# One decoder layer on one core: the ones of the squares from every head group, the fourth sum of x formed beside the second, and the first covering gate tile woven into the end of stick-breaking

## The chip, the core and the metric

The kernel runs on one core of a Trainium2 chip. The metric is the device time of one execution in microseconds (us). PE is TensorE, DVE is VectorE, ACT is ScalarE, POOL is GpSimd and SP is SyncE, which here issues DMAs.

## The reference

Hidden size 1024, 2048 tokens with 16 meta tokens ahead of them, one layer. Cut to its core:

```python
xn = rms_norm(h, norm_gain)
sb_q, sb_k, sb_v, sw_q, sw_k, sw_v, sb_z, sw_z, g_sb, g_sw = split(xn @ w_in)
o_sb = stick_breaking_attention(sb_q, sb_k, sb_v, valid)      # 8 heads of 64
o_sw = sliding_window_sink_attention(rope(sw_q), rope(sw_k), sw_v, sinks, valid)  # 16 heads, 2 of k and v, window 128
y_sb = (o_sb * silu(sb_z)) @ w_branch_sb
y_sw = (o_sw * silu(sw_z)) @ w_branch_swa
merged = sigmoid(g_sb) * y_sb + sigmoid(g_sw) * y_sw
h = h + merged @ w_out
return rms_norm(h, final_norm_gain)[:, BLOCK:]
```

Stick-breaking attention weighs key s for query t by sigmoid(z) times the product of (1 − sigmoid(z)) over the keys between them. Everything is in float32.

## The kernel before

**Numbers and tiles.** A float32 value is split into a high and a low part that PE can multiply at full rate; a product is three matmuls (high·high, low·high, high·low) of 128x128 weights on 128x512 values. `gemm` (L415 to L417) issues them for one column tile of 128 outputs and one group of 512 tokens: 8 steps of the inner dimension, so 24 matmuls into one PSUM bank. The banks are asked for by letter: g, z and t have two buffers each, o and zm one each. A buffer that is asked for again must first have been read by whoever uses its old content.

**Stages.** The tokens are worked in two halves of two groups each, first groups 2 and 3 ("half 0"), then 0 and 1 ("half 1"). In a half come the sliding window with the projections woven in, then stick-breaking attention with gate tiles woven in, then "pairs". A gate tile (`gate`, L583 the sigmoid, which empties the bank) is one column tile of the gates or of z, for both groups: two half-tiles of 24 matmuls, in this stage both in bank g.

**Stick-breaking** (`stick`) is a generator. Per step it makes scores (L1063, bank z), their sigmoid (ACT, L1066), a running product (DVE scans, L1073 and L1075), and five steps later (LT) transposes the rows on PE (L1091, bank t; of the meta tokens L1101). The transposed weights leave bank t split into a high part (ACT, wth, L115) and a low part (DVE, wtl, L116), and then multiply the values (L1122, bank o; of the meta tokens L1116, bank zm). When a head is done, L1126 (ACT) copies the result and L1127 and L1129 (DVE) add it up. `weave` issues one triple of gate matmuls after so much of the stick's work, in proportion to a ratio worked out from costs, so that PE always has something to do while ACT and DVE work.

**Squares.** In half 0, the stick also sums the squares of x for the tokens of the other half (ACT, L1041, two for a head group), into which a column of ones goes as a scale. It is made on POOL (L1080) from the last product row, so that the scheduler can't move the squares ahead of that row. It comes after every second head group; two buffers hold the loaded pieces of x (xq).

**Pairs.** The remaining gate tiles go two at a time by a scheme of seven products in place of eight (`gate_pair`, `seven`, PE L688). It needs sums of quarters of x, t1 to t4 (`sums_of_x`): L601 adds the high and the low part of a piece, L614, L615 and L617 make t3, t2 and t1, and each sum is split in two: L606 the cast on ACT, L607 the rest on DVE. t4 is made in a second phase by two subtractions (L626, L627), and its split stands inside the first pair (`between`). While the sums are made, PE works on covering tiles: 3 gate tiles in half 0 and 2 in half 1, each with the first group's half-tile in bank g and the second's in bank z. Ahead of the pairs their weights are made of sums too (`pair_weights`, L650 to L658).

**What sets the order.** PE's order is the order in which the program is written, by hand. DVE's is written by hand in the start and in the first pair. The order on ACT, DVE and POOL is otherwise set by the framework's scheduler; at run time each engine takes its list in order, and an instruction that waits holds up what follows it.

Of the kernel before, what the change touches and what calls it, by code (L numbers as in the profile page):

```python
# [12 lines left out]
ALU = mybir.AluOpType  # L13
# [6 lines left out]
KT = D // P  # L20
# [8 lines left out]
PLAIN = 18  # L29
# [4 lines left out]
HS = True  # L34
SR = (1.05, 1.09)
ULAG = 3
AB = 6
QW = 6.0
C_SBQ, C_SBK, C_SBV, C_SWQ, C_SWK, C_SWV, C_SBZ, C_SWZ, C_GSB, C_GSW = (
# [3 lines left out]
def f32(ap):  # L43
    return ap.bitcast(F32)
# [3 lines left out]
def tile_kernel(ctx, tc, x, xt, meta, metat, gain, w_in, w_sb, w_sw, w_out, sinks, fgain,  # L48
# [6 lines left out]
    V, A, G, T = nc.vector, nc.scalar, nc.gpsimd, nc.tensor  # L55
# [74 lines left out]

    clock = [0.0]

    def weave(main, side, ratio, credit=0.0):

        for c in main:
            clock[0] += c
            credit = min(credit + c * ratio, 6.0)
            while credit > 0:
                n = next(side, None)
                if n is None:  # L140
                    credit = float("-inf")
                    break
                if n == 0:
                    credit = 0.0
                    break
                credit -= n
        return credit
# [5 lines left out]
    def drain(*gens):  # L153
        for _ in chain(*gens):
            pass
# [433 lines left out]
    def sums_of_x(bp, groups):  # L589

        g, g2 = groups
        b = {"11": (g, 0), "12": (g2, 0), "21": (g, KT // 2), "22": (g2, KT // 2)}
        q = {n: [t[i][:, k:k + KT // 2, :] for t in (xh, xl)] for n, (i, k) in b.items()}
        for t in ("s4h", "s4l"):
            bp.tile([P, KT // 2, P], F32R, tag=t, name=t, bufs=2)
        for n in ("t4", "t1", "t3", "t2"):
            q[n] = [bp.tile([P, KT // 2, GT], F32R, tag=n + e, name=n + e) for e in "hl"]

        def whole(n, k):
            t = tmp()  # L600
            V.tensor_tensor(t, f32(q[n][0][:, k, :]), f32(q[n][1][:, k, :]), op=ALU.add)  # L601
            return t

        def parted(n, k, t):
            h, l = (u[:, k, :] for u in q[n])
            A.copy(h, t)  # L606
            V.tensor_tensor(l, t, f32(h), op=ALU.subtract)  # L607

        ks = range(KT // 2)
        held = [], []  # L610
        for k in ks:
            b11, b12, b22 = (whole(n, k) for n in ("11", "12", "22"))
            t3, t1 = ring_x(), ps(("t", "t", "o", "zm")[k])
            V.tensor_tensor(t3, b22, b12, op=ALU.subtract)  # L614
            V.tensor_tensor(b22, t3, b11, op=ALU.add)  # L615
            parted("t2", k, b22)
            V.tensor_tensor(t1, b12, b11, op=ALU.subtract)  # L617
            held[0].append(t1)
            held[1].append(t3)
        yield q  # L620
        for n, ts in zip(("t1", "t3"), held):
            for k in ks:
                parted(n, k, ts[k])
        for k in ks:
            b21, (t2h, t2l) = whole("21", k), (f32(t[:, k, :]) for t in q["t2"])
            V.tensor_tensor(b21, b21, t2h, op=ALU.subtract)  # L626
            V.tensor_tensor(b21, b21, t2l, op=ALU.subtract)  # L627
            held[0].append(b21)
        yield q
        for k, t in zip(ks, held[0][KT // 2:]):  # L630
            parted("t4", k, t)
        yield q

    def pair_weights(bp, ca, cb, plain):
# [44 lines left out]
            w[n], w[n2] = ([u[:, c] for u in t] for c in (lo, hi))  # L679
        return w  # L680

    def seven(w, b, tag, use, lead, between):

        def product(acc, n, m, first, last):
            (wh, wl), (bh, bl) = w[n], b[m]
            for k in range(KT // 2):
                for i, (l, r) in enumerate(((wh, bh), (wh, bl), (wl, bh))):
                    T.matmul(acc, lhsT=l[:, k, :], rhs=r[:, k, :], start=first and k == i == 0,  # L688
                             stop=k == KT // 2 - 1 and i == 2, skip_group_check=not (first and last))
        a0, p1 = ps("g"), tmp()  # L690
        product(a0, "11", "11", True, lead)
        A.copy(p1, a0)
        if lead:
            a3 = ps(tag)
            product(a3, "12", "21", True, True)
            t = tmp()
            V.tensor_tensor(t, a3, p1, op=ALU.add)
        yield
        a1, a2 = ps("z"), ps("t")
        u2, u3 = tmp(), tmp()  # L700
        product(a1, "s2", "t2", True, False)
        V.tensor_tensor(u2, a1, p1, op=ALU.add)
        if lead:
            between()
            use(0, 0, t)
            yield
        else:
            product(a0, "12", "21", False, True)
            use(0, 0, a0)
        a3 = ps(tag)  # L710
        product(a2, "s1", "t1", True, False)
        product(a1, "s3", "t3", False, True)
        V.tensor_tensor(u3, a1, p1, op=ALU.add)
        product(a3, "22", "t4", True, True)
        V.tensor_tensor(p1, a2, u3, op=ALU.add)
        V.tensor_tensor(u3, a3, u3, op=ALU.add)
        use(1, 1, p1)
        use(1, 0, u3)
        yield
        product(a2, "s4", "22", False, True)  # L720
        V.tensor_tensor(u2, a2, u2, op=ALU.add)
        use(0, 1, u2)

    def gate_pair(bp, ga, gb, groups, q, tag, plain, lead, between):
        tiles = ga, gb

        def use(m, n, t):
            c0, dst, silu, src = tiles[m]
            e = tmp()
            A.activation(e, t, AF.Sigmoid)  # L730
            if silu:
                V.tensor_tensor(e, t, e, op=ALU.mult)
            o = ring_x()
            DMA(o, src[groups[n]])
            V.tensor_tensor(e, e, o, op=ALU.mult)
            DMA(dst[groups[n]], e)
        w = yield from pair_weights(bp, ga[0], gb[0], plain)
        yield
        yield from seven(w, q, tag, use, lead, between)

    def in_line(pairs):

# [20 lines left out]
    def tiles_by_tile(makes, groups, meta=False):  # L763
        for mk in makes:
            w, use, wants = mk()
            for n, g in enumerate(reversed(groups) if wants == "back" else groups):
                yield from lagged(col_tile(w, g, use, meta and wants and n == 0))
# [212 lines left out]
    def stick(groups, bp, squared=()):  # L980
# [53 lines left out]
        def row(h, g, n, j):  # L1034
# [40 lines left out]
                V.tensor_tensor_scan(r[:, :w], r[:, :w], r[:, :w], last[j], op0=ALU.mult, op1=ALU.min)  # L1075
            last[j] = r[:, w - 1:w]
            rows_of[h, g, n, j] = r
            if end and n and j == 3 and squared:
                ones[0] = bp.tile([P, 1], F32, tag="one", name="one", bufs=4)
                G.tensor_scalar(ones[0], r[:, w - 1:w], 0.0, 1.0, op0=ALU.mult, op1=ALU.add)  # L1080
            if end:
# [52 lines left out]
        n = len(steps)  # L1134
# [187 lines left out]
    for half, groups in enumerate(halves):  # L1322
# [42 lines left out]
        with tc.tile_pool(name=f"sb{half}", bufs=1, side="left") as bp:  # L1365
            hsplit[0] = vsplit[0] = True
            next_sums = {g: sums() for g in halves[1]} if half == 0 else {}
            side = stick(groups, bp, [(x[g * GT + i * P:g * GT + (i + 1) * P, f * GT:(f + 1) * GT], ssq[:, f, i:i + 1])
                                      for g, ssq in next_sums.items() for i in range(4) for f in range(2)])
            ahead = 3 - half  # L1370
            drain(tiles_by_tile(gts[1:ahead], groups))
            rest, pairs0 = REST[half]
            cost_sb = 8 * sum(4 * (4 - g) for g in groups) * 1.31 + 8 * 0.75
            ratio = cost_sb / ((rest - ahead) * 10.4)
            weave(tiles_by_tile(gts[ahead:rest], groups), side, ratio)
            drain(side)
        with tc.tile_pool(name=f"pairs{half}", bufs=1, side="left") as bp:
            ts = [mk() for mk in gts[rest:pairs0]]
            sums_q = sums_of_x(bp, groups)
            tq = next(sums_q)  # L1380
            for n, (w, use, _) in enumerate(ts):
                for i, g in enumerate(groups):
                    drain(lagged(col_tile(w, g, use, bank="gz"[i])))
            order = gss[half]
            todo = in_line([gate_pair(bp, order[n], order[n + 1], groups, tq, ("o", "zm")[n // 2 % 2],
                                      half == 0 and n < PLAIN, n == pairs0, lambda: next(sums_q)) for n in range(pairs0, 26, 2)])
            next(todo)
            next(sums_q)
            for n in todo:
                if half == 0 and n == 4:  # L1390
                    t, u = (tmp()[:, :8] for _ in range(2))
                    for n, ssq in enumerate(next_sums.values()):
                        V.tensor_tensor(t[:, 4 * n:4 * n + 4], ssq[:, 0], ssq[:, 1], op=ALU.add)
                    rs = tp.tile([P, 8], F32, tag="rs8", name="rs", bufs=1)
                    rsqrt(rs, t, tp, t=u)
                    rs0, rs1 = rs[:, :4], rs[:, 4:]
# [71 lines left out]
```

## Time and profile before

| | us |
|---|---|
| three runs | 2107.55, 2111.84, 2111.94 (median 2111.84) |
| the profiled execution's own time | 2109.8 |
| its span, first to last instruction | 2108.1 |
| PE busy | 2082.2 |
| DVE busy | 1498.1 |
| ACT busy | 1081.1 |
| POOL busy | 183.6 |

A row of a timeline has the start, the duration, the engine, the line, the operation and the tiles (written <- read), and in brackets how long the engine was idle before it and for what. Matmuls overlap, so the distance of two starts counts there, not the duration. A row of the list of waits has who waited, on whom, the total, the number of times and the longest.

### The profile page before, as it was taken

How to read it: one execution, taken by the hardware profiler on the slowest of the kernel's cores; microseconds unless marked ns; L12 is line 12 of the kernel's file. 1: busy time of each engine (PE TensorE's matmuls, PEld its weight loads, DVE VectorE, ACT ScalarE, POOL GpSimd, SP SyncE). 2: the span in 40 equal slices, each digit the busy share in tenths (PEclk: the TensorE clock that was granted, in tenths of full speed). 3: DMA queues.
4: the chain of work that ended last, by engine and by line, in shares of the span. 5: the costliest groups of instructions: out<-in, count | busy, mean ns of one | idle time of the engine just before them, and what ended most of it. 6: DMA issues, size and time to landing. Idle time of an engine off the chain costs nothing.

```text
span 2108.1 us, 29921 instructions
## 1 busy us (share of the span) xinstructions
PE 2082.2 (99%) x10414; PEld 1732.7 (82%) x10414; DVE 1498.1 (71%) x2393; ACT 1081.1 (51%) x2442; POOL 183.6 (9%) x381
## 2 busy tenths in 40 slices
PE   8999999999999999999999999999999999999998
PEld 6788888888878888888888888888888888888887
DVE  7798885687898743877749989999994436543553
ACT  6677775576643434777745666666641312320121
POOL 2122331100100000122210000000000000000000
PEclk9999999999999999999999999999999999999999
DMA  9855455766448974444465333333248886547532
GB/s 339 293 183 187 175 181 183 246 210 190 136 173 298 354 270 155 151 160 141 140 196 155 114 111 94 117 121 100 86 150 299 277 314 201 191 163 252 159 110 80
DMA packets 179702, 392.96 MB, mean 186 GB/s; under 512 B 23296, under 2 KB 41536, under 8 KB 179552
## 3 DMA queue, kind: packets, MB, share of 16 engines
q1 hardware_dynamic: 179552, 391.06, 54.7%
q8 instruction: 82, 1.34, 0.3%
q14 instruction: 68, 0.56, 0.1%
HBM read 243.64 MB, written 147.28 MB: 185 GB/s over the span
## 4 chain that ended last, share of the span: by engine, by line
PE 91%; DVE 4%; DMA 2%; ACT 2%; issue 1%; SPq 0%; POOL 0%; DVEq 0%; ACTq 0%
PE ps_g L415 12%; PE ps_g L416 12%; PE ps_g L417 12%; PE ps_o L1122 6%; PE ps_t L1091 5%; PE ps_z L1063 5%; PE ps_z L898 3%; PE ps_o L944 3%; PE ps_t L688 2%; PE ps_z L688 2%; PE ps_g L688 2%; PE ps_g L236 1%; PE ps_g L237 1%; PE ps_g L238 1%; PE ps_z L236 1%; PE ps_z L237 1%
## 5 line engine op out<-in xcount | busy, mean ns | idle before, releaser
L415 PE MATMUL ps_g<-xh,wh 128*128 128x512 f32 x1184 | 483.8, 409 | 7.3 <-ACT xh L1174 7.1
L416 PE MATMUL ps_g<-xl,wh 128*128 128x512 f32 x1184 | 465.1, 393 | 0.0
L417 PE MATMUL ps_g<-xh,wl 128*128 128x512 f32 x1184 | 464.5, 392 | 0.0
L417 PEld LDWEIGHTS ps_g<-xh,wl 128*128 128x128 f32 x1184 | 222.8, 188 | 49.6
L415 PEld LDWEIGHTS ps_g<-xh,wh 128*128 128x128 f32 x1184 | 223.5, 189 | 43.8 <-ACT xh L1174 7.1
L416 PEld LDWEIGHTS ps_g<-xl,wh 128*128 128x128 f32 x1184 | 224.0, 189 | 35.6 <-DVE xl L1175 1.3
L1066 ACT ACTIVATE row<-ps_z 128x512 f32<-128x512 f32 (+2 forms) x320 | 165.4, 517 | 144.4 <-PE ps_z L1063 140.9
L1075 DVE TENSOR_TENSOR_SCAN row<-row 128x528 f32<-128x528 f32 (+1 forms) x192 | 210.5, 1097 | 15.4 <-ACT row L1066 11.8
L115 ACT ACTIVATE wth<-ps_t 128x512 fp32r<-128x512 f32 (+1 forms) x320 | 170.5, 533 | 68.4 <-PE ps_t L1091 65.5
L116 DVE SCALAR_TENSOR_TENSOR wtl<-ps_t,wth 128x512 fp32r<-128x512 f32 (+1 forms) x320 | 189.5, 592 | 18.4 <-ACT wth L115 17.5
L1073 DVE TENSOR_TENSOR_SCAN row<-row,mask 128x512 f32<-128x512 f32 (+4 forms) x128 | 144.3, 1130 | 52.1 <-ACT row L1066 51.4
L1091 PE MATMUL ps_t<-ident,row 128*128 128x128 f32 x1088 | 171.9, 273 | 4.2 <-DVE wtl L116 3.4
L1063 PE MATMUL ps_z<-kt,q 128*128 128x512 f32 (+4 forms) x608 | 170.3, 355 | 0.0
L1091 PEld LDWEIGHTS ps_t<-ident,row 128*128 128x128 f32 x1088 | 134.6, 140 | 40.7 <-DVE wtl L116 6.6
L1122 PE MATMUL ps_o<-wth,vc 128*128 128x512 f32 (+1 forms) x320 | 133.4, 417 | 0.0
L1063 PEld LDWEIGHTS ps_z<-kt,q 128*128 128x128 f32 x608 | 111.0, 188 | 19.9
L906 ACT ACTIVATE sc<-sc,nm 128x129 f32<-128x129 f32 x256 | 100.0, 393 | 39.7 <-DVE nm L904 38.8
L1122 PE MATMUL ps_o<-wtl,vc 128*128 128x512 f32 (+1 forms) x320 | 117.2, 366 | 0.2
L112 DVE TENSOR_TENSOR wl<-raw,wh 128x1024 fp32r<-128x1024 f32 (+1 forms) x51 | 58.2, 1142 | 45.1 <-ACT wh L109 40.2
L1082 POOL COPY xs<-row 128x16 f32<-128x16 f32 x128 | 29.7, 232 | 598.9 <-DVE row L1075 533.9
L301 ACT ACTIVATE sq<-res 128x512 bf16<-128x512 f32 x32 | 20.2, 632 | 116.5 <-DVE res L297 116.4
L898 PEld LDWEIGHTS ps_z<-kk,q 128*128 128x128 f32 x512 | 69.8, 190 | 6.4 <-DVE q L879 0.7
(417 smaller groups left out, 4180.0 us busy)
## 6 DMA issues: line engine op xcount, KB each, us to landing
wh<-h_in_w_in SPq DMA_DIRECT2D x58, 512.0 KB
wl<-l_in_w_in SPq DMA_DIRECT2D x58, 512.0 KB
raw<-in_w_in SPq DMA_DIRECT2D x50, 512.0 KB
h_in_w_in<-wh SPq DMA_DIRECT2D x40, 512.0 KB
l_in_w_in<-wl SPq DMA_DIRECT2D x40, 512.0 KB
q<-qd SPq DMA_DIRECT2D x120, 128.0 KB
vc<-vd SPq DMA_DIRECT2D x48, 256.0 KB
kd<-tmp SPq DMA_DIRECT2D x32, 256.0 KB
```

Of the source, the lines that this page charges most:

```text
L115: A.activation(h, acc, AF.Copy, scale=scale)
L116: V.scalar_tensor_tensor(l, acc, scale, f32(h), op0=ALU.mult, op1=ALU.subtract)
L415: T.matmul(acc, lhsT=wh[:, k, :], rhs=xh[g][:, k, :], start=k == 0, stop=False)
L416: T.matmul(acc, lhsT=wh[:, k, :], rhs=xl[g][:, k, :], start=False, stop=False)
L417: T.matmul(acc, lhsT=wl[:, k, :], rhs=xh[g][:, k, :], start=False, stop=k == KT - 1)
L898: T.matmul(acc[:, a * 256:(a + 1) * 256], lhsT=lq, rhs=kk[:, 2 * kv + hl, blk * P:(blk + 2) * P], start=hl == 0, stop=hl == 1)
L1063: T.matmul(acc[:, :b - a], lhsT=lq, rhs=kt[h][:, k0 + a:k0 + b], start=t == 0, stop=t == 1)
L1066: A.activation(r[:, a:b], acc[:, :b - a], AF.Sigmoid, scale=-1.0)
L1073: V.tensor_tensor_scan(r[:, :w], r[:, :w], mask[0][:, :w], 1.0, op0=ALU.mult, op1=ALU.max)
L1075: V.tensor_tensor_scan(r[:, :w], r[:, :w], r[:, :w], last[j], op0=ALU.mult, op1=ALU.min)
L1091: T.transpose(tr[:, j * P:(j + 1) * P], rows_of[h, g, n - (j > i), j][:, k0:k0 + P], ident)
L1122: T.matmul(o[:, :n], lhsT=v, rhs=r, start=first and r is wh, stop=last and r is wl)
```

## The change

It has three parts; line numbers after it differ a little, and L586 of the changed kernel is the sigmoid L583 of the kernel before, L609 the cast L606, L604 the sum L601, L618 the sum L615 (of t2), L610 the split L607, L418 to L420 the matmuls L415 to L417, L1088 the transposes L1091 and L1119 the products L1122.

- Ones: the column of ones is made at the end of every head group (16 times, not 8), and each two squares take the ones of the group that has just ended.
- Fourth sum: t4 = b21 − b22 is formed in the first phase of the sums, next to t2 (one subtraction in place of two), and split there. `between` goes.
- Cover: the first covering tile joins the tiles that are woven into the stick. The ratio counts 0.2 of a tile more, `weave` ends when the stick does (`rest`), and what is left of the tile is issued after the sums' first phase has been written, ahead of the other covering tiles. The tile is now made by the function of the woven tiles, so that both of its half-tiles ask for bank g.

```diff
+COVER = 0.2
...
-    def weave(main, side, ratio, credit=0.0):
+    def weave(main, side, ratio, credit=0.0, rest=False):
...
                 if n is None:
+                    if rest:
+                        return
                     credit = float("-inf")
                     break
...
             parted("t2", k, b22)
             V.tensor_tensor(t1, b12, b11, op=ALU.subtract)
+            b21 = whole("21", k)
+            V.tensor_tensor(b21, b21, b22, op=ALU.subtract)
+            parted("t4", k, b21)
...
-        for k in ks:
-            b21, (t2h, t2l) = whole("21", k), (f32(t[:, k, :]) for t in q["t2"])
-            V.tensor_tensor(b21, b21, t2h, op=ALU.subtract)
-            V.tensor_tensor(b21, b21, t2l, op=ALU.subtract)
-            held[0].append(b21)
-        yield q
-        for k, t in zip(ks, held[0][KT // 2:]):
-            parted("t4", k, t)
         yield q
...
         if lead:
-            between()
             use(0, 0, t)
...
-            if end and n and j == 3 and squared:
+            if end and j == 3 and squared:
                 ones[0] = bp.tile([P, 1], F32, tag="one", name="one", bufs=4)
...
-            ratio = cost_sb / ((rest - ahead) * 10.4)
-            weave(tiles_by_tile(gts[ahead:rest], groups), side, ratio)
+            ratio = cost_sb / ((rest - ahead + COVER) * 10.4)
+            cover = tiles_by_tile(gts[ahead:rest + 1], groups)
+            weave(cover, side, ratio, rest=True)
             drain(side)
         with tc.tile_pool(name=f"pairs{half}", bufs=1, side="left") as bp:
-            ts = [mk() for mk in gts[rest:pairs0]]
+            ts = [mk() for mk in gts[rest + 1:pairs0]]
             sums_q = sums_of_x(bp, groups)
             tq = next(sums_q)
+            drain(cover)
```

The order of PE at the end of the stick in half 1, before. ps_t is the bank of the last transposes, ps_o that of the products with the values, ps_g that of the first covering tile:

```order
L1091 MATMUL ps_t_17261<-ident_66,row_17181 128x128
L1122 MATMUL ps_o_17026<-wth_17229,vc_16582 128x512
L1122 MATMUL ps_o_17026<-wtl_17230,vc_16582 128x512
L1122 MATMUL ps_o_17026<-wth_17247,vc_16582 128x512
L1122 MATMUL ps_o_17026<-wtl_17248,vc_16582 128x512
L1116 MATMUL ps_zm_17274<-wm0_71,vm_70 128x512
L1122 MATMUL ps_o_17026<-wth_17266,vc_16582 128x512
L1122 MATMUL ps_o_17026<-wtl_17267,vc_16582 128x512
L415 MATMUL ps_g_17359<-xh_8558,wh_17289 128x512
```

The same place of the changed kernel:

```order
L1088 MATMUL ps_t_17290<-ident_66,row_17206 128x128
L1119 MATMUL ps_o_17052<-wth_17259,vc_16603 128x512
L1119 MATMUL ps_o_17052<-wtl_17260,vc_16603 128x512
L418 MATMUL ps_g_17214<-xh_8570,wh_17210 128x512
L419 MATMUL ps_g_17214<-xl_8571,wh_17210 128x512
L420 MATMUL ps_g_17214<-xh_8570,wl_17211 128x512
L1119 MATMUL ps_o_17052<-wth_17273,vc_16603 128x512
L1119 MATMUL ps_o_17052<-wtl_17274,vc_16603 128x512
L1113 MATMUL ps_zm_17306<-wm0_71,vm_70 128x512
L1119 MATMUL ps_o_17052<-wth_17295,vc_16603 128x512
L1119 MATMUL ps_o_17052<-wtl_17296,vc_16603 128x512
L418 MATMUL ps_g_17214<-xh_8570,wh_17210 128x512
```

The covering tile's first half-tile (ps_g_17214) is begun among the stick's last steps; of its 24 matmuls and the 24 of the second half-tile, 33 are left when the stick has ended (30 in half 0).

The order of PE at the border of the first covering tile to the second, half 1, before: the last matmuls of the first tile's second half-tile and the first of the second tile:

```order
L415 MATMUL ps_z_17387<-xh_8671,wh_17289 128x512
L416 MATMUL ps_z_17387<-xl_8672,wh_17289 128x512
L417 MATMUL ps_z_17387<-xh_8671,wl_17290 128x512
L415 MATMUL ps_g_17415<-xh_8558,wh_17293 128x512
L416 MATMUL ps_g_17415<-xl_8559,wh_17293 128x512
L417 MATMUL ps_g_17415<-xh_8558,wl_17294 128x512
```

And changed:

```order
L418 MATMUL ps_g_17419<-xh_8683,wh_17210 128x512
L419 MATMUL ps_g_17419<-xl_8684,wh_17210 128x512
L420 MATMUL ps_g_17419<-xh_8683,wl_17211 128x512
L418 MATMUL ps_g_17447<-xh_8570,wh_17324 128x512
L419 MATMUL ps_g_17447<-xl_8571,wh_17324 128x512
L420 MATMUL ps_g_17447<-xh_8570,wl_17325 128x512
```

The half-tiles went through banks g, z, g (ps_g_17359, ps_z_17387, ps_g_17415) and now go through g, g, g (ps_g_17214, ps_g_17419, ps_g_17447), and g has two buffers.

The order of ACT there, before. L606 are the casts of the sums, L583 the sigmoid that empties a half-tile's bank:

```order
L606 CAST t1h_17301<-ps_t_17314 128x512
L606 CAST t3h_17303<-xs_17313 128x512
L606 CAST t1h_17301<-ps_t_17327 128x512
L606 CAST t2h_17305<-tmp_17311 128x512
L606 CAST t3h_17303<-xs_17326 128x512
L606 CAST t1h_17301<-ps_o_17340 128x512
L606 CAST t2h_17305<-tmp_17324 128x512
L583 ACTIVATE tmp_17384<-ps_g_17359 128x512
```

And changed:

```order
L609 CAST t1h_17332<-ps_t_17345 128x512
L609 CAST t3h_17334<-xs_17344 128x512
L609 CAST t2h_17336<-tmp_17342 128x512
L609 CAST t1h_17332<-ps_t_17363 128x512
L609 CAST t4h_17330<-tmp_17351 128x512
L609 CAST t3h_17334<-xs_17362 128x512
L609 CAST t2h_17336<-tmp_17360 128x512
L609 CAST t4h_17330<-tmp_17369 128x512
L609 CAST t1h_17332<-ps_o_17381 128x512
L609 CAST t3h_17334<-xs_17380 128x512
L609 CAST t2h_17336<-tmp_17378 128x512
L586 ACTIVATE tmp_17416<-ps_g_17214 128x512
```

The sigmoid of the first half-tile stood behind seven casts and stands behind eleven; the last of them needs the third t2 (L618), which is the 36th of DVE's instructions from the first L604 (in half 0 the 40th, with the same eleven casts ahead). The second t2 is the 23rd (27th in half 0).

More of the change, by code (lines that the diff above doesn't have):

```diff
@@ L680, in pair_weights, with seven @@
         return w
-    def seven(w, b, tag, use, lead, between):
+    def seven(w, b, tag, use, lead):
         def product(acc, n, m, first, last):
@@ L722, in seven, with gate_pair @@
         use(0, 1, u2)
-    def gate_pair(bp, ga, gb, groups, q, tag, plain, lead, between):
+    def gate_pair(bp, ga, gb, groups, q, tag, plain, lead):
         tiles = ga, gb
@@ L738, in gate_pair @@
         yield
-        yield from seven(w, q, tag, use, lead, between)
+        yield from seven(w, q, tag, use, lead)
     def in_line(pairs):
@@ L1385, in tile_kernel @@
             todo = in_line([gate_pair(bp, order[n], order[n + 1], groups, tq, ("o", "zm")[n // 2 % 2],
-                                      half == 0 and n < PLAIN, n == pairs0, lambda: next(sums_q)) for n in range(pairs0, 26, 2)])
+                                      half == 0 and n < PLAIN, n == pairs0) for n in range(pairs0, 26, 2)])
             next(todo)
```

## Prediction

> **What bounds the kernel now.** I read the page first, then TensorE's list of waits, then the timelines of PE, DVE and ACT at the two places that the diff touches. From the page:
>
> ```profile
> span 2108.1 us, 29921 instructions
> PE 2082.2 (99%) x10414; PEld 1732.7 (82%) x10414; DVE 1498.1 (71%) x2393; ACT 1081.1 (51%) x2442; POOL 183.6 (9%) x381
> PE 91%; DVE 4%; DMA 2%; ACT 2%; issue 1%; SPq 0%; POOL 0%; DVEq 0%; ACTq 0%
> ```
>
> PE is busy for 99% of the span, and the chain that ended last is 91% PE. The change keeps the number of matmul rows, so all that it can save is PE's idle time, and what it can lose is any idle time that it adds. The list of PE's waits says how little there is to save:
>
> ```profile
> PE ps_g L415 <- ACT xh L1174: 7.1, 1, 7.1
> PE ps_t L1091 <- DVE wtl L116: 3.4, 5, 1.4
> PE ps_t L1101 <- DVE wtl L116: 2.7, 2, 2.5
> PE ps_t L688 <- DVE tmp L715: 1.0, 1, 1.0
> PE ps_t L688 <- DMA wl<-p2l: 0.3, 1, 0.3
> ```
>
> Columns are total, times and longest. The 7.1 us are the start, which the change leaves alone. The three rows on DVE's wtl and tmp, 7.1 us together, are what the change can reach. So the question is what it adds.
>
> The profiled execution took 2109.8 us by its own time, 1.7 us more than its span; the median of the three runs is 2111.84, 2.0 above. I make the sum on 2109.8. Differences under 0.2%, about 4.2 us, count as no change.
>
> **The end of the stick in half 1 (L1091 to the cover), PE:**
>
> ```profile
> 1542.59 0.66 PE L1091 MATMUL ps_t<-ident,row 128*128 128x128 f32 x4 [0.51 <-DVE wtl L116]
> 1544.24 0.40 PE L1122 MATMUL ps_o<-wth,vc 128*128 128x512 f32 x1
> 1544.75 0.50 PE L1122 MATMUL ps_o<-wtl,vc 128*128 128x512 f32 x1
> 1545.09 0.40 PE L415 MATMUL ps_g<-xh,wh 128*128 128x512 f32 x1
> 1550.55 0.39 PE L415 MATMUL ps_z<-xh,wh 128*128 128x512 f32 x1
> 1555.99 0.39 PE L415 MATMUL ps_g<-xh,wh 128*128 128x512 f32 x1
> 1566.87 0.39 PE L688 MATMUL ps_g<-xh,wh 128*128 128x512 f32 x1
> ```
>
> The last four transposes start at 1542.59; I count from there and call it T. The first covering tile is one half-tile of 24 matmuls in bank g (1545.09) and one in bank z (1550.55); the second tile takes g again at 1555.99, in g's other buffer. A matmul takes (1566.87 − 1545.09)/96 = 0.227 us. Nothing stalls. Now the two engines beside it, DVE and then ACT:
>
> ```profile
> 1544.61 3.09 DVE L601 TENSOR_TENSOR tmp<-xh,xl 128x512 f32<-128x512 f32 x5
> ...
> 1557.61 0.68 DVE L615 TENSOR_TENSOR tmp<-xs,tmp 128x512 f32<-128x512 f32 x1
> ...
> 1569.65 0.68 DVE L607 TENSOR_TENSOR t2l<-tmp,t2h 128x512 fp32r<-128x512 f32 x1
> ```
>
> ```profile
> 1557.74 0.59 ACT L606 CAST t1h<-ps_o 128x512 fp32r<-128x512 f32 x1 [1.19 <-DVE ps_o L617]
> 1558.33 0.62 ACT L606 CAST t2h<-tmp 128x512 fp32r<-128x512 f32 x1
> 1559.61 0.60 ACT L583 ACTIVATE tmp<-ps_g 128x512 f32<-128x512 f32 x1 [0.66 <-DVE xs L614]
> ```
>
> DVE goes over to the sums of x at 1544.61, and 41 operations later it is at 1569.65, so 0.611 us each. The row at 1559.61 is the one that matters: it is the sigmoid that empties the half-tile that PE finished at about 1550.5. It ran 9 us late, because ACT takes its list in order and seven casts of the sums, each waiting for DVE, stand ahead of it. Before the change that lateness is free: no matmul wants that buffer soon.
>
> **The cover's banks, the part that I expect to decide.** In the changed order the first covering tile takes bank g for both half-tiles (g has two buffers), so the first matmul of the next tile needs the buffer of half-tile A and must wait for its sigmoid (L586 there). On ACT that sigmoid stands behind eleven casts, the last of them t2h of the third sum, which waits for DVE's L618, the 36th operation from the first L604.
>
> Half 1, from T. PE: the four transposes 0.41, then 2 ps_o matmuls 0.46, 3 of the gate 0.68, 2 ps_o 0.46, ps_zm 0.23, 2 ps_o 0.46, then the 33 matmuls left of the tile, 33 × 0.227 = 7.49: PE stands at the next tile at T + 10.2. DVE: first sum at 1544.61 − 1542.59 = 2.02, the 36th starts 35 × 0.611 = 21.4 later, at T + 23.4; its cast starts 0.72 after it (1557.61 to 1558.33), the sigmoid some 0.55 behind the cast, and it takes 0.60: T + 25.3. **Stall 25.3 − 10.2 = 15.1 us.** I allow 14.4 to 15.6, by DVE at 0.60 or 0.62 each.
>
> Half 0 is the same with more in it:
>
> ```profile
> 587.10 0.69 DVE L116 SCALAR_TENSOR_TENSOR wtl<-ps_t,wth 128x512 fp32r<-128x512 f32 x1 [0.66 <-ACT wth L115]
> 587.71 3.96 DVE L601 TENSOR_TENSOR tmp<-xh,xl 128x512 f32<-128x512 f32 x5
> 602.79 1.22 DVE L651 TENSOR_TENSOR wl<-raw,wh 128x1024 fp32r<-128x1024 f32 x1
> 603.92 0.69 DVE L617 TENSOR_TENSOR ps_o<-tmp 128x512 f32<-128x512 f32 x1
> 610.54 0.68 DVE L615 TENSOR_TENSOR tmp<-xs,tmp 128x512 f32<-128x512 f32 x1
> ```
>
> ```profile
> 585.78 0.66 PE L1091 MATMUL ps_t<-ident,row 128*128 128x128 f32 x4 [1.43 <-DVE wtl L116]
> 587.42 0.39 PE L1122 MATMUL ps_o<-wth,vc 128*128 128x512 f32 x1
> 587.85 0.50 PE L1122 MATMUL ps_o<-wtl,vc 128*128 128x512 f32 x1
> ```
>
> T is 585.78. PE reaches the next tile at 0.41 + 0.68 + 0.94 + 0.68 + 0.23 + 0.46 = 3.40 (two more gate triples stand there) plus 30 × 0.227 = 6.8: T + 10.2 again. DVE starts the sums right behind the last wtl (587.10), at 587.71 − 585.78 = 1.93, and now 0.6 later because one L652 now stands ahead of the last wtl. The third L618 is the 40th operation, and one of the 39 ahead of it is a 1024-wide split that takes 603.92 − 602.79 = 1.13; the others start 0.602 apart (11 from 603.92 to 610.54). So 38 × 0.602 + 1.13 = 24.0, start at T + 26.5, cast 0.72 on, sigmoid 0.55 behind it and 0.60 long: T + 28.4. **Stall 18.2 us**, 17.4 to 19.2. What else ACT has ahead of it (a 1024-wide cast, some 1 us) hides in ACT's waits for DVE.
>
> **PE after a long idle.** No idle of 15 us stands in this trace except by the start; a shorter one is in the middle:
>
> ```profile
> 7.06 0.80 PE L415 MATMUL ps_g<-xh,wh 128*128 128x512 f32 x1 [7.06 <-ACT xh L1174]
> ...
> 12.26 0.60 PE L416 MATMUL ps_g<-xl,wh 128*128 128x512 f32 x1
> 12.69 0.41 PE L417 MATMUL ps_g<-xh,wl 128*128 128x512 f32 x1
> 12.93 0.39 PE L415 MATMUL ps_g<-xh,wh 128*128 128x512 f32 x1
> ```
>
> ```profile
> 487.96 0.60 PE L1101 MATMUL ps_t<-ident,xs 128*32 128x128 f32 x4 [2.48 <-DVE wtl L116]
> 488.63 0.39 PE L416 MATMUL ps_g<-xl,wh 128*128 128x512 f32 x1
> 488.86 0.40 PE L417 MATMUL ps_g<-xh,wl 128*128 128x512 f32 x1
> ```
>
> After 7.06 us of idle the matmuls come 0.43 us apart (12.26 to 12.69) and only from 12.69 on 0.23. The 11 between 7.06 and 12.69 took 5.63 where 2.50 is the full rate: 3.1 lost, part of it perhaps loads; at 0.43 each, 11 × 0.20 = 2.2. After 2.48 us of idle (488.63 to 488.86) there is no loss. Stalls of 15 and 18 us are nearer to the first: I take 2.2 each, so 4.4, and from 0 to 6.2 for both.
>
> The Trainium skill's TensorE: Matmul & The Clock Gate (Part 1: The HAM clock gate (the "warmup" mystery)) says that the clock halves after an idle window of about 3.4 us and comes back after as long under load. By that page alone I would estimate 1.7 us per stall, 3.4 together, and the sum below would be 1.0 lower; both rows agree with where it puts the limit.
>
> **What the change saves.** *Tails.* In half 0 PE idles 1.43 and, between 587.42 and 587.85, 0.2 more. Now gate matmuls stand between, but a weight split stands ahead of a wtl (its price is 1.13) and I expect some 1.0 of idle there: −0.7 (0 to −1.6). In half 1 it idles 0.51 and 0.28 (1544.24 to 1544.75). Gate triples of 0.68 now stand ahead of both; the last wtl ended at T + 2.0, and PE gets to it at T + 2.2: −0.8 (0 to −0.8).
>
> *t4.* Four subtractions go (t4 = b21 − b22 in one step each) and the split moves out of the first pair. That frees the DVE list ahead of the stall of the first pair (1.0 in the list, DVE tmp L715); what is late next there is a weight load from DRAM (0.3 in the list): −0.8 (0 to −1.0). The cost, four subtractions and four splits earlier, is in the 36 and the 40 above.
>
> *Ones.* The squares of x now come two per head group with their own ones, instead of four close together after every second:
>
> ```profile
> ACT xq L1041 <- POOL one L1080: 4.9, 5, 1.2
> ACT xq L1041 <- DMA xq<-in_x: 3.5, 3, 2.5
> 485.02 0.72 ACT L1041 ACTIVATE xq<-xq,one 128x512 f32<-128x512 f32 x1 [2.51 <-DMA xq<-in_x]
> ```
>
> ACT idles 2.51 before the square at 485.02, since the second two of such a bunch wait for their load; the wth behind it is late, DVE's wtl too, and PE idles the 2.48 at 487.96. Spread out, the load has a head group's time. I take −2.5; the bounds are 0 and −4.2 (the rows L1101 and L1091 on wtl, 2.7 + 3.4, less the 1.9 of them counted with the tails). The eight more GpSimd instructions cost nothing: POOL is 9% busy, and who waits for them is ACT alone. Each could add a wait of the kind of the 4.9 us in five; these hid, as PE's list shows.
>
> **Sum.** 2109.8 + 18.2 + 15.1 + 4.4 − 0.7 − 0.8 − 0.8 − 2.5 = **2142.7 us**.
>
> **Rivals.**
> 1. *The eviction is not held up* (0.06): the place is the sigmoid L586 of half-tile A on ACT, the price the two stalls and the slow restarts, 37.7 us. It decides if the sigmoid ends within T + 10.2. Then only the savings are left: 2109.8 − 4.8 = 2105.0, faster. For it: PE's list of before has no wait on a sigmoid. Against it: the casts of two sums and three of the third's stand ahead on ACT, and the row at 1559.61 shows ACT keeping to its order while PE's half-tile lay ready.
> 2. *Both stall, but by half* (0.06): if the third t2h is not what the sigmoid waits for, but the second (23rd operation in half 1, T + 2.0 + 22 × 0.611 + 1.9 = 17.3; 27th in half 0, T + 20.5), the stalls are 7.1 and 10.3: 2109.8 + 17.4 + 4.4 − 4.8 = 2126.8. For it: in before the sigmoid stood right behind such a second t2h (1558.33, 1559.61). Against it: ACT's order as it now stands.
> 3. *The change does nothing that can be measured* (0.03): the cover's B goes to another bank after all and the savings meet waits of the same size next: 2109.8.
> 4. *Both stalls, as forecast* (0.85), from 2109.8 + 17.4 + 14.4 − 7.6 = 2134 to 2109.8 + 19.2 + 15.6 + 6.2 = 2151. The runs lie 2.3 below to 2.1 above the profiled one: 2132 to 2153.
>
> **The numbers.** The likeliest is 4, so 2142.7. Range 2130 to 2153: 4's own range and the two us between it and a DVE list that is three operations shorter at the waiting place; it leaves out 1, 2 and 3, 0.15. Slower by over 0.2%: 2 and 4, 0.91; within 0.2%: 3 and a third of 1 (2105.0 lies just beyond 4.2 below), 0.05; faster: 0.04.
>
> **What would show it.** In the profile after: PE's waits lead with two long ones of ps_g on ACT's tmp (L586), 18 and 15 us; ahead of each PE takes 30 to 33 gate matmuls after the stick's last ps_o without a gap, and behind it some 11 to 16 matmuls at 0.43. ACT's L586 comes right behind the t2h cast. The wait of L1038 on xq's load is gone. I am wrong if ps_g has no long wait, or if PE goes on after it at once at full rate (then 4.4 less).

## The result, and the profile after

| | before, us | after, us |
|---|---|---|
| median beside each other | 2109.74 (4 runs, 2107.55 to 2111.94) | 2146.95 (4 runs, 2146.17 to 2147.84) |
| profiled execution, own time | 2109.8 | 2146.53 |
| span | 2108.1 | 2144.8 |

The ratio is 1.0176, with a 95% interval of 1.016 to 1.0192: slower, inside the range of 2130 to 2153 and 4.2 us above the forecast of 2142.7.

Two rows of the page of the changed kernel:

```profile
span 2144.8 us, 29910 instructions
PE 2087.3 (97%) x10414; PEld 1736.2 (81%) x10414; DVE 1494.4 (70%) x2385; ACT 1079.6 (50%) x2442; POOL 189.0 (9%) x389
```

PE has as many instructions as before and is busy 5.1 us longer, over a span that is 36.7 longer. So some 32 us are new idle time (34.7 in two new waits, less some 3 in the others), and the 5 are matmuls that took longer. PE's waits, longest in total first:

```profile
PE ps_g L418 <- ACT tmp L586: 34.7, 2, 19.7
PE ps_g L418 <- ACT xh L1171: 6.5, 1, 6.5
PE ps_t L1088 <- DVE wtl L117: 6.0, 8, 1.5
```

The first row was not in the list of before: PE waits twice, 34.7 us in all, for the sigmoid that empties bank g. The row on tmp of the first pair (1.0 before) is gone. The one on wtl has grown from 3.4 to 6.0, but the other row on wtl (L1101, 2.7 before) is gone too, so that PE waits for wtl as long as before, 6.0 for 6.1.

Half 1, PE: the last transposes (T = 1565.60), the last matmul of the first covering tile, and the first ones of the second tile.

```profile
1565.60 0.64 PE L1088 MATMUL ps_t<-ident,row 128*128 128x128 f32 x4
...
1575.69 0.39 PE L420 MATMUL ps_g<-xh,wl 128*128 128x512 f32 x1
1591.05 0.80 PE L418 MATMUL ps_g<-xh,wh 128*128 128x512 f32 x1 [14.97 <-ACT tmp L586]
1591.64 0.63 PE L419 MATMUL ps_g<-xl,wh 128*128 128x512 f32 x1
1592.07 0.63 PE L420 MATMUL ps_g<-xh,wl 128*128 128x512 f32 x1
...
1595.48 0.59 PE L419 MATMUL ps_g<-xl,wh 128*128 128x512 f32 x1
1595.91 0.40 PE L420 MATMUL ps_g<-xh,wl 128*128 128x512 f32 x1
1596.14 0.40 PE L418 MATMUL ps_g<-xh,wh 128*128 128x512 f32 x1
```

DVE and ACT in the same stretch:

```profile
1567.74 3.09 DVE L604 TENSOR_TENSOR tmp<-xh,xl 128x512 f32<-128x512 f32 x5
...
1589.17 0.68 DVE L618 TENSOR_TENSOR tmp<-xs,tmp 128x512 f32<-128x512 f32 x1
```

```profile
1589.88 0.62 ACT L609 CAST t2h<-tmp 128x512 fp32r<-128x512 f32 x1 [1.78 <-DVE tmp L618]
1590.41 0.59 ACT L586 ACTIVATE tmp<-ps_g 128x512 f32<-128x512 f32 x1
```

This is the chain of the forecast link by link: the third L618 on DVE, its cast on ACT, the sigmoid right behind it, and PE goes on at 1591.05, T + 25.4. It had stood since T + 10.5 (1591.05 less the 14.97). ACT was idle for 1.78 ahead of that cast: the half-tile lay ready all that time, and ACT waited for DVE in front of it.

Half 0, PE and then DVE and ACT:

```profile
582.81 0.66 PE L1088 MATMUL ps_t<-ident,row 128*128 128x128 f32 x4 [1.46 <-DVE wtl L117]
...
587.60 0.64 PE L1088 MATMUL ps_t<-ident,row 128*128 128x128 f32 x4
...
597.94 0.39 PE L420 MATMUL ps_g<-xh,wl 128*128 128x512 f32 x1
618.01 0.79 PE L418 MATMUL ps_g<-xh,wh 128*128 128x512 f32 x1 [19.69 <-ACT tmp L586]
...
622.87 0.51 PE L420 MATMUL ps_g<-xh,wl 128*128 128x512 f32 x1
623.21 0.40 PE L418 MATMUL ps_g<-xh,wh 128*128 128x512 f32 x1
```

```profile
588.22 0.69 DVE L651 TENSOR_TENSOR s<-raw 128x512 f32<-128x512 f32 x1 [0.69 <-DMA raw<-in_w_in]
...
590.86 3.96 DVE L604 TENSOR_TENSOR tmp<-xh,xl 128x512 f32<-128x512 f32 x5
...
616.13 0.68 DVE L618 TENSOR_TENSOR tmp<-xs,tmp 128x512 f32<-128x512 f32 x1
```

The third L618 starts at T + 28.5 where the forecast had T + 26.5, and PE's wait is longer by most of that. After each wait twelve matmuls take 5.20 us (618.01 to 623.21) and 5.09 us (1591.05 to 1596.14); at 0.227 each they would take 2.72. That is 2.5 and 2.4 us.

The account, from the starts on PE's timelines of the two kernels: waits +34.7, slow matmuls +4.9, the pairs −1.3 (half 0: 115.27 us from the first to the last L688 before, 114.01 after) and −0.8 (half 1: 76.82 and 75.99), the stretch up to the stick −1.0, half 1's last steps −0.2. That makes 36.3 of the 36.7.

### The profile page after: what moved, and what is told of

It reads as the page before. It is cut to its first block, busy times and chain, and to the rows that moved or that the text cites. A ratio compares the mean times of both kernels' runs of the same rounds, so it can differ in the third digit from the quotient of the medians.

```text
span 2144.8 us, 29910 instructions
## 1 busy us (share of the span) xinstructions
PE 2087.3 (97%) x10414; PEld 1736.2 (81%) x10414; DVE 1494.4 (70%) x2385; ACT 1079.6 (50%) x2442; POOL 189.0 (9%) x389
## 4 chain that ended last, share of the span: by engine, by line
PE 68%; DVE 3%; ACT 1%; issue 0%; DVEq 0%; ACTq 0%
PE ps_g L418 7%; PE ps_g L419 7%; PE ps_g L420 7%; PE ps_o L1119 4%; PE ps_t L1088 4%; PE ps_z L1060 4%; PE ps_t L686 3%; PE ps_z L686 3%; PE ps_g L686 2%; PE ps_g L239 1%; PE ps_g L240 1%; PE ps_g L241 1%; PE ps_z L239 1%; PE ps_z L241 1%; PE ps_z L240 1%; PE ps_z L895 1%
## 5 line engine op out<-in xcount | busy, mean ns | idle before, releaser
L418 PE MATMUL ps_g<-xh,wh 128*128 128x512 f32 x1200 | 495.7, 413 | 41.4 <-ACT tmp L586 34.7
L419 PE MATMUL ps_g<-xl,wh 128*128 128x512 f32 x1200 | 473.1, 394 | 0.0
L420 PE MATMUL ps_g<-xh,wl 128*128 128x512 f32 x1200 | 472.4, 394 | 0.0
L418 PEld LDWEIGHTS ps_g<-xh,wh 128*128 128x128 f32 x1200 | 227.8, 190 | 78.6 <-ACT tmp L586 35.5
L420 PEld LDWEIGHTS ps_g<-xh,wl 128*128 128x128 f32 x1200 | 226.9, 189 | 51.1
L419 PEld LDWEIGHTS ps_g<-xl,wh 128*128 128x128 f32 x1200 | 228.3, 190 | 35.3 <-DVE xl L1172 1.3
L1088 PE MATMUL ps_t<-ident,row 128*128 128x128 f32 x1088 | 172.3, 274 | 6.8 <-DVE wtl L117 6.0
L1088 PEld LDWEIGHTS ps_t<-ident,row 128*128 128x128 f32 x1088 | 133.5, 140 | 42.9 <-DVE wtl L117 9.8
L1119 PE MATMUL ps_o<-wth,vc 128*128 128x512 f32 (+1 forms) x320 | 129.7, 405 | 0.0
L1119 PE MATMUL ps_o<-wtl,vc 128*128 128x512 f32 (+1 forms) x320 | 116.9, 365 | 0.0
```

The costliest lines, as they stand in the source:

```text
L418: T.matmul(acc, lhsT=wh[:, k, :], rhs=xh[g][:, k, :], start=k == 0, stop=False)
L419: T.matmul(acc, lhsT=wh[:, k, :], rhs=xl[g][:, k, :], start=False, stop=False)
L420: T.matmul(acc, lhsT=wl[:, k, :], rhs=xh[g][:, k, :], start=False, stop=k == KT - 1)
L1088: T.transpose(tr[:, j * P:(j + 1) * P], rows_of[h, g, n - (j > i), j][:, k0:k0 + P], ident)
L1119: T.matmul(o[:, :n], lhsT=v, rhs=r, start=first and r is wh, stop=last and r is wl)
```

## The experiments

Theory A: PE waits because the first half-tile's sigmoid is late, behind the casts of the sums, and everything counts that moves the sigmoid or PE's next want of its buffer. Theory B: the sharing of bank g by both half-tiles is the whole cost. Each expectation stands as it was written before the run.

**The second half-tile in bank z.**

```diff
+            cover = chain(tiles_by_tile(gts[ahead:rest], groups), tiles_by_tile(gts[rest:rest + 1], groups, banks="gz"))
-            cover = tiles_by_tile(gts[ahead:rest + 1], groups)
```

> The changed kernel with the second half-tile of the woven covering tile in bank z instead of g. Theory A (a late sigmoid): the sigmoid of the first half-tile still ends 30.4 us (half 0) and 25.5 us (half 1) after the last transposes, only the buffer is wanted again 48 matmuls or 10.9 us later, so that PE waits 19.8 - 10.9 = 8.9 us and 15.1 - 10.9 = 4.2 us: 2147 - 21.8 = about 2125 us, 2 to 5 less if the matmuls behind such shorter waits are not slow. Theory B (the collision of both half-tiles in bank g is the whole of it): no wait is left, 2147 - 34.9 - 4.9 = 2107 us.

2126.62 us (1.0082 of the kernel before, with the interval 1.0066 to 1.0097; so also below). PE's waits:

```profile
PE ps_g L418 <- ACT tmp L586: 9.3, 1, 9.3
PE ps_g L686 <- ACT tmp L586: 4.1, 1, 4.1
```

9.3 and 4.1 where theory A had 8.9 and 4.2, and still for the sigmoid: the other bank gives PE 48 more matmuls until it wants the buffer, no more. In half 1 it is the first pair (L686) that wants it then. Theory B falls.

**The fourth sum late again**, ones and cover as changed.

```diff
-            b21 = whole("21", k)
-            V.tensor_tensor(b21, b21, b22, op=ALU.subtract)
-            parted("t4", k, b21)
...
+        for k in ks:
+            b21, (t2h, t2l) = whole("21", k), (f32(t[:, k, :]) for t in q["t2"])
```

> The changed kernel with the fourth sum made in the second phase and split in the first pair, as before; ones and cover as changed. Theory A: the first half-tile's sigmoid stands behind seven casts again, the last of them the second t2, so the waits shrink to about 12 us in half 0 and 7.3 us in half 1, and the 2 us that the pairs had gained go: 2147 - 15.4 + 2 = about 2134 us. Theory B (only the banks count): the waits stay, 2149 us.

2133.36 us (1.0115, 1.01 to 1.013).

```profile
PE ps_g L418 <- ACT tmp L586: 19.9, 2, 12.5
...
PE ps_t L691 <- DVE tmp L718: 1.0, 1, 1.0
```

12.5 and 7.4 us, against 12 and 7.3 expected: of the 34.7 us the fourth sum's place in the first phase makes 14.8, with banks as changed. The old wait of the first pair is back, which shows that the early fourth sum does take it away.

**The fourth sum alone**, on the kernel before.

```diff
             V.tensor_tensor(t1, b12, b11, op=ALU.subtract)
+            b21 = whole("21", k)
+            V.tensor_tensor(b21, b21, b22, op=ALU.subtract)
+            parted("t4", k, b21)
...
-            between()
             use(0, 0, t)
```

> The kernel before with the fourth sum alone changed: formed and split in the first phase, no split in the first pair; covering tiles and ones as before. Theory A (a late sigmoid): the first phase now has eleven casts ahead of the first covering tile's sigmoid; in half 0 it ends about 31 us after the last transposes, while PE wants that buffer for the third tile at 24.3: 6.6 us of wait and some 2 us at the slow rate; in half 1 PE waits about 1.0 for the buffer and 0.7 for bank zm; the pairs gain 2.1: 2109 + 8 = about 2117 us. Theory B (the early fourth sum only saves DVE work): 2109 - 2 = 2107 us.

2119.77 us (1.0043, 1.0029 to 1.0057).

```profile
PE ps_g L415 <- ACT tmp L583: 7.1, 1, 7.1
...
PE ps_g L683 <- ACT tmp L583: 0.9, 1, 0.9
```

So that part alone, with the banks of before, makes the kernel slower: 7.1 us for the sigmoid in half 0, 1.7 at the slow rate behind it, and 0.9 for the sigmoid in half 1. The pairs save 1.3 us in half 0 (114.01 us against 115.27); in half 1 a wait of 0.7 for bank zm uses the gain up (77.15 against 76.82). The stick of half 0 is 1.6 us longer, by slow matmuls that the last section shows. In the kernel before that sigmoid ended 2.9 us ahead of PE's want (it started at 606.51 and took 0.60, and the third tile began 96 matmuls after 588.18, at 610.0); four sums' casts and splits ahead of it use that up.

**The rest of the covering tile ahead of the sums.**

```diff
             sums_q = sums_of_x(bp, groups)
+            drain(cover)
             tq = next(sums_q)
-            drain(cover)
```

> The changed kernel with the rest of the covering tile written ahead of the sums, both half-tiles in bank g: ACT has the first half-tile's sigmoid, and the second's too, ahead of the casts of the sums. Theory A: no wait for bank g is left; the casts of the sums start behind the second sigmoid, some 4 to 5 us later, and PE waits for the second sum instead at the first pair, about 7 us in half 1 and 4 in half 0: 2118 to 2123 us. Theory B: both half-tiles still share bank g, so about 2147 us.

2129.80 us (1.01, 1.0083 to 1.0117), above the 2118 to 2123 of theory A.

```profile
PE ps_zm L686 <- DVE t1l L610: 13.3, 1, 13.3
...
PE ps_g L686 <- ACT tmp L586: 3.9, 1, 3.9
```

No matmul of a covering tile waits for bank g any more, with the banks as changed, so the order on ACT is enough for that; the 3.9 us are the first pair of half 0. But the sums pay: their casts stand behind the two sigmoids, and the first pair wants bank zm, in which the fourth piece of t1 lies until it is split (L610). I had half 1's wait at the second sum and half as long; the bank had escaped me.

**The first half-tile ahead of the sums, the second behind and in bank z.**

```diff
+            cover = chain(tiles_by_tile(gts[ahead:rest], groups), half_tile(0, "g"))
...
+            drain(cover)
             tq = next(sums_q)
-            drain(cover)
+            drain(half_tile(1, "z"))
```

> The changed kernel with the first half-tile's rest written ahead of the sums and the second half-tile behind their first phase and in bank z, so that the first sigmoid stands ahead of all casts of the sums on ACT. Theory A: no wait for bank g; what is late next is the second sum's last split on DVE in half 1, at T + 32.0 where PE wants it at T + 28.6: 3.4 us of wait, so 2109.7 - 2.3 + 3.4 = about 2111 us. Rival: that split is hidden, and only the savings are left, 2107 us.

2124.45 us (1.0074, 1.0059 to 1.0089), 13 above what theory A expected.

```profile
PE ps_zm L686 <- DVE t1l L610: 7.4, 1, 7.4
...
PE ps_z L418 <- ACT tmp L586: 5.0, 1, 5.0
```

Bank g is free, as expected. What is late next is not what I named: again bank zm, and in half 0 the second half-tile's sigmoid. Each wait had its slow matmuls behind it.

**The same with the fourth sum late** (the edits of this run and of the second one together).

> The weave and the ones of the changed kernel, but the first half-tile's rest written ahead of the sums, the second half-tile in bank z, and the fourth sum late as before. Theory A (the weaving costs nothing by itself, it only brings the wants of PE forward by 12 to 15 matmuls): no wait for g, z or zm is left, the pairs lose the 2.1 us, about 2109 us, as the kernel before. Rival: weaving the tile in costs or saves by itself, over 2112 or under 2106 us.

2114.61 us (1.0018, 1.001 to 1.0027): 3.7 above the kernel before, so theory A's "costs nothing" is off and the rival's "over 2112" holds, though no large wait is left:

```profile
PE ps_t L691 <- DVE tmp L718: 1.9, 1, 1.9
PE ps_z L691 <- DVE t2l L610: 1.4, 1, 1.4
PE ps_zm L691 <- DVE t1l L610: 0.8, 1, 0.8
PE ps_z L691 <- DVE tmp L705: 0.7, 1, 0.7
```

These 4.8 us, of which 1.0 stood in the kernel before, are all DVE's. By PE's timeline the pairs are what is longer, by 0.9 us in half 0 and 3.5 in half 1. The stick takes 12 of the 48 matmuls ahead of T and 3 to 6 more behind it; these are 3.4 us in half 1 that PE no longer has to spend while DVE makes the sums, which fits the 3.5.

**The ones alone**, on the kernel before, and **the changed kernel without them**.

```diff
-            if end and n and j == 3 and squared:
+            if end and j == 3 and squared:
```

> The kernel before with the ones made after every head group, nothing else changed. Theory A (from the trace after: the waits for xq's load went, but the squares wait for their ones as often): no change, 2109 us within 1. Theory B (my step in the prediction): 2109 - 2.5 = 2106.5 us.

2107.95 us against 2110.87 (11 and 21 runs): 0.9988, 0.9979 to 0.9997, so 0.6 to 4.4 us faster. So the prediction's step exists, against theory A of this run. Its 2.5 lies in that interval; the trace shows 1.4 of it in the stick. It is also the one version that beats both kernels. ACT's waits and the square that PE had waited for:

```profile
ACT xq L1041 <- POOL one L1080: 6.9, 7, 1.4
```

```profile
484.97 0.72 ACT L1041 ACTIVATE xq<-xq,one 128x512 f32<-128x512 f32 x1 [1.36 <-POOL one L1080]
```

The waits for the load of xq are gone (3.5 us before), those for the ones are longer (4.9 before), and the longest fell from 2.5 to 1.4.

> The changed kernel with the ones made after every second head group, as before. Theory A (the ones save 1.4 to 2.5 us by themselves, and the woven tile's other gate triples take as much from the stick elsewhere): 2147 + 2 = about 2149 us, with PE's wait of 2.5 us on the xq load back. Theory B (the ones save nothing where the tile is woven in): 2147 us within 1.

2147.08 us against 2146.95 of the changed kernel (1.0174 of the kernel before, 1.016 to 1.0188): nothing, as theory B has it. PE's wait of 2.5 us isn't back either, though ACT waits 3.3 us for the loads of xq again: PE waits 0.3 us there, and for wtl elsewhere 5.4 us in eight places (3.4 in five before). So the weave by itself takes the long wait away and adds others.

By PE's timeline the stick of half 0, from its first scores to T, takes 202.88 us before and 201.49 with the ones alone. With the tile woven in, 12 matmuls (2.72 us) more stand in it; less these it takes 202.34 with the ones as before and 203.03 in the changed kernel. So the ones shorten the stick by 1.4 us without the woven tile and lengthen it by 0.7 with it. The total doesn't show the 0.7: the run with the ones as before was 1.7 us later at the start of the stick and lost 1.2 less at the slow rate behind the two long waits.

**PE kept busy in the wait.** The changed kernel with 78 and 60 matmuls ahead of the second covering tile whose product nobody reads.

```diff
             drain(cover)
+            fill, count = ps("z"), 78 - 18 * half
+            for k in range(count):
+                T.matmul(fill, lhsT=xh[groups[0]][:, 0, :P], rhs=xh[groups[0]][:, 0, :], start=k == 0, stop=k == count - 1)
```

> The changed kernel with 78 (half 0) and 60 (half 1) matmuls of no use put in front of the second covering tile, into a buffer of bank z that nobody reads: they take 17.7 and 13.6 us of the 19.8 and 15.1 that PE waits for the sigmoid. Theory A (PE runs slowly after a long idle because it was idle): the sigmoid comes when it did, the rest of the wait is 1 to 2 us, and the 4.9 us of slow matmuls go: 2147 - 4.9 = 2142 us. Rival (the slow matmuls come from what DVE and ACT do just then): still 2147 us.

2143.19 us (1.0154 of the kernel before, 1.0138 to 1.0169), 3.8 below the changed kernel where 4.9 was expected.

```profile
616.26 1.29 PE L1382 MATMUL ps_z<-xh 128*128 128x512 f32 x5
619.57 0.50 PE L418 MATMUL ps_g<-xh,wh 128*128 128x512 f32 x1 [2.01 <-ACT tmp L586]
619.91 0.40 PE L419 MATMUL ps_g<-xl,wh 128*128 128x512 f32 x1
620.15 0.40 PE L420 MATMUL ps_g<-xh,wl 128*128 128x512 f32 x1
620.38 0.40 PE L418 MATMUL ps_g<-xh,wh 128*128 128x512 f32 x1
```

The sigmoid comes when it did, and the matmuls behind it are 0.34 and then 0.23 apart. So the idle time made them slow, not the work of DVE and ACT. By PE's timeline the stretches from T to the first pair are 2.3 and 2.2 us shorter than in the changed kernel, 4.5 of the 4.9; this execution was 1.6 us later at the start of the stick, ahead of all that the filling touches.

**Ones and fourth sum without the woven tile**, the first covering half-tile ahead of the sums.

```diff
+            drain(lagged(col_tile(ts[0][0], groups[0], ts[0][1], bank="g")))
             tq = next(sums_q)
```

> The kernel before with the ones and the fourth sum changed, no woven covering tile, and the first half-tile of the first covering tile written ahead of the sums, so that its sigmoid stands ahead of the casts. Theory A: the 7.1 us wait of the run with the fourth sum alone goes; what is late next is the second half-tile's sigmoid (bank z) in half 0, 1.5 us, and the first sum in bank zm in half 1, 1.7 us; with 1.4 saved by the ones and 2.1 in the pairs that is 0.3 us under the kernel before, no change. Rival: with that sigmoid out of the way all the savings stay, 3.5 us under the kernel before.

2117.23 us (1.0038, 1.0024 to 1.0052), where I expected no change.

```profile
PE ps_zm L683 <- DVE t1l L607: 4.3, 1, 4.3
PE ps_z L415 <- ACT tmp L583: 3.2, 1, 3.2
```

```profile
1551.65 0.60 ACT L583 ACTIVATE tmp<-ps_g 128x512 f32<-128x512 f32 x1 [4.88 <-PE ps_g L417]
1552.60 0.59 ACT L606 CAST t1h<-ps_t 128x512 fp32r<-128x512 f32 x1 [0.35 <-DMA od<-xs]
```

The waits are the two that I named, at 4.3 and 3.2 us for 1.7 and 1.5, and 1.7 us of slow matmuls behind each, which the expectation did not count. A sigmoid that is put ahead of the casts holds the casts up in turn: ACT is idle 4.88 us for the half-tile's matmuls, and the first cast comes after them. Bank zm waits for what that delays.

## Why the prediction was right, step by step

- **The step that decides held.** The buffer of bank g, the sigmoid behind eleven casts, the third L618: the trace shows each link, and moving the buffer's next want (bank z) or shortening the list (fourth sum late) changed both waits to within 0.5 us of what the step gives.
- **Half 1's wait**: 15.1 forecast, 15.0 measured. **Half 0's**: 18.2 forecast, 19.7 measured, beyond the 19.2 that the prediction allowed. Two sizes were off there. The sums start at T + 3.3 and not at T + 2.5, since a second weight operation (L651) stands ahead of the last wtl and waited 0.69 us for its load; and I put the first five sums at 0.602 each, 3.0, though the row of before that I quoted has 3.96.
- **PE after the wait**: 2.2 each forecast, 2.5 and 2.4 measured.
- **Tails**: in half 1 the two waits (0.8) are gone, but the stick gained only 0.2 in all. In half 0 I expected 0.7; the wait has moved from the last transposes to those at 582.81 and is as long as before (1.46 for 1.43).
- **Fourth sum in the pairs**: 0.8 forecast, 2.1 measured, as half 1's pairs gained too. The 1.3 of half 0 come back in the other runs; half 1's 0.8 is less sure, as its pairs vary by some 0.7 between like runs. The prediction counted its cost only through the 36 and the 40. That was right in size, but it did not say that this part is slower by itself, with no tile woven in.
- **Ones**: −2.5 forecast; in the changed kernel nothing is saved. This is the term that failed. It put the saving on PE's wait of 2.48 at L1101, as if the stick's order stayed. But the ratio of the weave places the gate triples anew, and that by itself takes this wait away and adds others for wtl (from 3.4 to 5.4 us, and to 6.0 with the ones). Without the weave the ones do save, 0.6 to 4.4.
- The profiled execution came 3.8 above the forecast of 2142.7: 1.4 of the waits, 0.5 of the slow matmuls, 2.5 of the ones, 0.7 and 0.6 of the tails, less 1.3 more from the fourth sum and 1.0 from the stretch up to the stick. That makes 3.4; 0.4 is not placed. The 1.0 is luck: the change doesn't touch that stretch, and the stick starts between 381.6 and 383.8 us in the runs here. The miss of the ones is small beside the two waits, so it did not show in the total.

Rival 1 (no wait) and rival 3 (no change) are out by the two waits; rival 2 (the second t2 decides) is what the run with the fourth sum late shows, at 12.5 and 7.4 us, and only there.

What stays open: why the ones lengthen the stick once the tile is woven in; and how the banks would have to lie for the early fourth sum to keep its 2 us. A version with bank o in the place of zm was not tried.

## What to carry to other kernels

A buffer comes free when its reader's turn comes on an engine that works in order, not when its content is ready: before a step asks for a buffer sooner, count what stands ahead of the reader on that engine, and what the last of it waits for. Work that covers another engine's phase has a size to keep; taking covering matmuls away and adding to the phase both draw on the same slack (2.9 us in half 0 here), and once that is gone the whole overrun is paid. Moving the reader ahead isn't free either, since what it passes then waits for the reader's own input.

## What the runs showed of the hardware

The price of an idle PE hardly depends on how long it was idle. Behind waits of 3.2 to 19.7 us, in eight of the kernels here, 6 to 12 matmuls came some 0.43 us apart, and 1.4 to 2.5 us were lost: 2.1 behind 9.3 us, 2.4 behind 4.1, 1.4 behind 5.0. The same wait of 19.7 us cost 2.5 us in the changed kernel and 1.7 in the one with the ones as before.

The granted clock in the traces (PEclk) shows what the price hangs on. The first row is the changed kernel's half 0, the second the run with the fourth sum alone:

```profile
core 0: us, PE busy (x) PEld busy (x) DVE busy (x) ACT busy (x) POOL busy (x), PEclk, DMA share, GB/s
602.62:623.10 20.48, 5.09 (x12) 4.03 (x13) 20.48 (x34) 8.20 (x15) 0.00 (x0) 0.50 0.24 88
488.73:492.14 3.41, 3.41 (x12) 2.82 (x11) 2.22 (x4) 1.84 (x4) 0.00 (x0) 0.50 0.97 291
```

In the first, the clock is half of full from 4.3 us after PE fell idle (598.33) until 5.09 us after it went on (618.01), and half of these 5.09 us is the 2.5 lost. Behind the waits of the eight kernels the clock came back 2.8 to 5.1 us after PE went on. These stretches at half clock, between the start and the end of the kernel, all last 3.413 us or a whole multiple of it (20.48 is six): the clock changes in steps of that length, and where in a step PE goes on decides what it loses.

A shorter idle time can do it too, and not at once. In the run with the fourth sum alone, PE waited 2.19 us and went on at full rate; the slow matmuls came a microsecond later, and lasted until the clock came back at 492.15:

```profile
487.54 0.60 PE L1095 MATMUL ps_t<-ident,xs 128*32 128x128 f32 x4 [2.19 <-DVE wtl L116]
...
488.21 0.40 PE L416 MATMUL ps_g<-xl,wh 128*128 128x512 f32 x1
488.44 0.39 PE L417 MATMUL ps_g<-xh,wl 128*128 128x512 f32 x1
...
491.17 0.63 PE L415 MATMUL ps_g<-xh,wh 128*128 128x512 f32 x1
491.59 0.63 PE L416 MATMUL ps_g<-xl,wh 128*128 128x512 f32 x1
492.02 0.46 PE L417 MATMUL ps_g<-xh,wl 128*128 128x512 f32 x1
```

In the kernel before, 2.48 us at the same place cost nothing. Counted in steps of 3.413 us, the wait of 2.19 us lies whole in the step that ends where the clock falls (485.32 to 488.73); that of 2.48 us (485.48 to 487.96) has a border in it, at 487.15, if the steps are counted from the rise of the clock at 12.70. That fits; how much idle time in a step is enough, these runs do not settle.

The Trainium skill (TensorE: Matmul & The Clock Gate, Part 1: The HAM clock gate (the "warmup" mystery)) states that the activity window is about 3.4 us long and free-running, so that the point at which the clock changes depends on where in the window the matmuls begin. The traces agree, with steps of 3.413 us. Its limit of about 3.4 us for an idle gap is not a safe distance: the 2.19 us above were enough.
